# Mixer of the last two blocks: three PSUM pools of two banks merged into one of six used in turn, scores of the differential attention two blocks ahead

## The chip, the cores and the metric

The kernel runs on one core of one Trainium2 chip. The metric is the device time of one execution in microseconds. TensorE multiplies matrices and writes into PSUM (eight banks of 128 x 512 fp32 numbers in this kernel); VectorE, ScalarE and GpSimd read the banks or work on SBUF; SyncE issues most of the DMAs.

## What is computed

Four transformer blocks on 512 tokens of width 1024 in fp32: two of a first kind (window attention with a gated linear attention, then retention) and two of a second kind. The change touches the mixer of the second kind, which runs twice. It has three branches beside each other: a convolution of 31 taps with a norm, a differential attention of six heads, and a gated delta rule of six heads in two directions. Cut to these:

```python
def diff_attention(q, k, v, lam..., subln_w, layer_idx):
    def block(args):                      # 128 queries against 512 keys
        s = jnp.einsum("bqmd,bkmd->bmqk", q_blk, kf)          # 2 x 6 maps, width 32
        p = jax.nn.softmax(s - slopes[:, None, None] * dist, axis=-1)
        p = p.reshape(B, H, 2, Q_BLOCK, S)
        a = p[:, :, 0] - lam * p[:, :, 1]
        return jnp.einsum("bhqk,bkhe->bqhe", a, vf)
    o = rms_norm_2(lax.map(block, ...), subln_w, eps=1e-5) * (1.0 - lambda_init)

def chunk_gated_delta(q, k, v, g, beta):  # chunks of 64 tokens
    A = jnp.where(strict, jnp.einsum("bhncd,bhnsd->bhncs", kb, kc) * decay, 0.0)
    sol = lax.linalg.triangular_solve(A, rhs, left_side=True, lower=True, unit_diagonal=True)
    u, w = sol[..., :Dv], sol[..., Dv:]
    def step(state, inp):
        v_new = u_i - jnp.einsum("bhcd,bhde->bhce", w_i, state)
        o = jnp.einsum("bhcd,bhde->bhce", qg_i, state) + jnp.einsum("bhcs,bhse->bhce", aqk_i, v_new)
        state = state * gl_i[..., None, None] + jnp.einsum("bhcd,bhce->bhde", kdec_i, v_new)
        return state, o

def second_block(x, ...):                 # for l in range(2)
    u = rms_norm_2(x, pre_mix_w[l]) @ w_in[l]                 # then split into the branches
    y = jnp.concatenate([conv_module(...), diff_attention(...), gated_deltanet(...)], axis=-1) @ w_out[l]
    x = x + rms_norm_2(y, post_mix_w[l])
    y = jnp.square(jax.nn.relu(rms_norm_2(x, pre_mlp_w[l]) @ w_ff1[l])) @ w_ff2[l]
    x = x + rms_norm_2(y, post_mlp_w[l])
```

## The kernel before

A product in fp32 is made of three: both operands are split into a high and a low part, and `mm3` issues high x high, high x low and low x high (lines 485 to 487). `wsplit` makes the two parts of a weight (tiles `wh` and `wl`); the split input is `hh` and `hl`. All rows of L485 to L487 are such dense products.

`second(l)` (line 1974) writes the mixer of one layer out as a program, and a tile scheduler makes the five engines' queues from it. The tiles of a pool share its buffers by tag: a tile may be written when an earlier one of its tag has been read for the last time, and tiles of one tag take the buffers in the order of the program. Beyond that an engine's queue can hold a later part of the program ahead of an earlier one. Before, the eight PSUM banks are four pools of two:

- `mm` (`psum`): dense products, the value products of the attention (`L509 mm<-dv,dat`), and the transposes after its norm (L1707).
- `fx` (`psf`): half of the gate projection, the transposes of the short convolution (L1400), and the attention's scores and transposes.
- `ax` (`psx`): everything of the delta rule but its running states, and the transposes of its output (also L1707).
- `sA`: the two running states of a scan.

The program of a mixer, with heads of the delta rule taken in three pairs f = 0, 1, 2:

1. The first projections and `gates`, then for each pair `delta_proj` (its q, k, v), `delta_prep` (products of keys, L1475, with decays, L1446 and L1463; the small triangular systems, `delta_solve`, 15 steps of two VectorE instructions on L1518 and L1520), and its second half, `rest`, on the queries. With them stand the projection and the 31 taps of the convolution (L1743, VectorE).
2. `uw(f)`: the 64 x 64 systems are built from the small ones. For each direction it is a chain TensorE, VectorE, TensorE and so on: L1559 and L1569/L1570 (32 x 32 products), L1571, L1583, an eviction, L1592, L1593, L1583 and L1592 again for the other half, then L1604 (products with values, 64 x 128).
3. `scan(f)`: 7 steps in each direction, a pair of 64 x 64 products into `sA` and a copy (L1650 on VectorE, L1652 on ScalarE) each, then the output's products (all on L509).
4. `out(f)`: a norm over VectorE, ScalarE and GpSimd, four transposes (L1707), an eviction and a DMA.
5. Dense projections of gate and values for tokens (`dense_tok`, 384 columns) and of the attention's q and k (`diff_proj`, 512 columns). The gate projection holds four accumulators at once, `banks = [psum, psum, psf, psf]`, and its weight stays split until the last of the four has used it.
6. `diff`: 24 blocks (six heads by four blocks of 128 queries). `scores(b)` writes two `fx` tiles (L1840), which VectorE takes out with the bias (L1842) and ScalarE exponentiates (L1844). `outputs(b)` combines the two maps (L1854 to L1862; the large step in two blocks of three on VectorE), transposes the result into a third `fx` tile (L1866), copies it out, and multiplies with the values into `mm`. Before, the loop is `scores(b + 1)` then `outputs(b)`. After every second head stand a norm and L1707; after the first of these the convolution's norm.

The order of the program is: proj 0, prep 0, rest 0, proj 1, prep 1, rest 1, projection of the convolution, uw 0, proj 2, taps, prep 2, scan 0, uw 1, gate projection, value projection, q and k projections, out 0, scan 1, rest 2, uw 2, out 1, scan 2, out 2, diff. After it the output projection `w_out` reads all branches.

Of the kernel before, what the change touches and what calls it, by code (L numbers as in the profile page):

```python
# [16 lines left out]
PSUM = bass.MemoryType.PSUM  # L17
# [104 lines left out]
class Rows:  # L122


    def __init__(self, a, b, c0=0, c1=768):
        self.t, self.c0, self.c1 = (a, b), c0, c1
# [32 lines left out]
class Slots:  # L159
# [6 lines left out]
    def tile(self, shape, dt, tag, name, bufs=1):  # L166
        n = int(np.prod(shape[1:]))
        if n < P:
            return self.pool.tile(shape, dt, tag=tag, name=name, bufs=bufs)
        t = self.slots[self.n % len(self.slots)][:, :n]  # L170
        self.n += 1
        names = "abcd"[:len(shape) - 1]
        return t.rearrange(f"p ({' '.join(names)}) -> p {' '.join(names)}", **dict(zip(names, shape[1:])))


class Kern:
# [1618 lines left out]
    def diff(self, l, pool, qk, vd, cat, between):  # L1795
# [31 lines left out]
        def scores(b):  # L1827
            hd, qb = b // 4, b % 4
            if qb == 0:
                head(hd)  # L1830
            s = heads[hd]
            if b % 2 == 0:
                blocks[b // 2] = (self.p_raw.tile([P, 2048], F32, tag="raw", name="dP").rearrange("p (q m c) -> p q m c", q=2, m=2),
                                  self.p_whl.tile([P, 1024], F32R, tag="wl", name="dat").bitcast(F32).rearrange("p (q k c) -> p q k c", q=2, k=4))
            pe = blocks[b // 2][0][:, b % 2]
            o0 = 384 - P * qb
            for m in range(2):
                ps = self.psf()
                t = s["qk"][m]
                nc.tensor.matmul(ps, t[:, qb * P:(qb + 1) * P], t[:, 512:], start=True, stop=True)  # L1840
                mx = s["mx"][:, qb, m:m + 1]
                nc.vector.tensor_tensor_reduce(out=pe[:, m], in0=ps, in1=s["bias"][:, o0:o0 + 512], scale=1.0, scalar=3.0e38,  # L1842
                                               op0=ALU.add, op1=ALU.min, accum_out=mx)
                nc.scalar.activation(pe[:, m], pe[:, m], AF.Exp, bias=mx, scale=-1.0, accum_out=s["sm"][:, qb, m:m + 1])  # L1844
            self.load["dve"] += 1300
            self.load["act"] += 1050
# [33 lines left out]

        nb = 24
        scores(0)
        for b in range(nb):
            if b + 1 < nb:
                scores(b + 1)
            outputs(b)

    def second_consts(self, pool, tmp):
# [85 lines left out]
    def second(self, l):  # L1974
        tc, nc, I = self.tc, self.nc, self.I
# [6 lines left out]
        qk = [pd.tile([2, 4, P, 512], F32, tag=f"qk{l}{f}", name="qk") for f in range(3)]  # L1982
        cat = pd.tile([P, KT, 512], F32, tag=f"cat{l}", name="cat")
        p_ps = ExitStack()
        self.pd, self.pf, self.px, psa = (p_ps.enter_context(tc.tile_pool(name=f"{t}{l}", bufs=2, space=PSUM))
                                          for t in ("mm", "fx", "ax", "sA"))
        p_cv, cv, p_hs = self.p_cv, self.cv, self.p_hs
        nc.sync.dma_start(xs, self.x)
        self.p_x.close()
# [2 lines left out]
        pool = p_dl.enter_context(tc.tile_pool(name=f"dl{l}", bufs=1))  # L1992
# [61 lines left out]
        with ExitStack() as st:  # L2054
# [24 lines left out]
            for k in range(KT):  # L2079
                t = p_f.tile([P, 4, 256], F32, tag="o", name="ct", bufs=2).rearrange("p a b -> p (a b)")[:, :512]  # L2080
# [20 lines left out]
    def mlp(self, l, pool, hs, y, evy, done):  # L2101
# [66 lines left out]
        for p in range(3, 16):  # L2168
            strassen(p)
            if p % 2 == 0 and p < 13:  # L2170
                second([p - 2, p - 1])
# [190 lines left out]
```

## Time and profile before

| what | us |
|---|---|
| median of 3 runs (lowest to highest) | 4025.6 (4014.26 to 4031.81) |
| the profiled execution | 4036.42 |
| its span | 4034.6 |
| first mixer, transpose of the gate rows to first product of the output projection | 420.2 |
| second mixer, the same | 418.3 |

Over the span TensorE is busy 92%, VectorE 60%, GpSimd 41%, ScalarE 39%. The line PEclk of the page cuts the span into 40 slices and shows the clock that TensorE was granted in tenths of its full speed of 2.4 GHz; a stretch with 0.50 is at the lower level of 1.2 GHz all the time, one with 0.75 half of it. In tables of stretches each engine has its busy time in us and, behind x, its instructions; PEld is the loading of weights into TensorE, which runs beside the products. Products are pipelined, so the durations of single ones overlap, and busy time is what counts for many in a row. Where a row names a releaser (`<-PE fx L1840`), it is what ended the idle time of the engine before these instructions.

### The profile page before, as it was taken

The page shows a single profiled execution, that of the slowest core. Times are in us where ns is not written, and L with a number is a line of the kernel's source. Part 1 is how long each engine was busy: PE and PEld are TensorE (multiplying, and loading weights), DVE is VectorE, ACT ScalarE, POOL GpSimd, SP SyncE. Part 2 cuts the span into 40 slices and gives each one's busy share as a digit, 9 for nine tenths or more (in the row PEclk, how much of TensorE's full clock was granted, in tenths as well). Part 3 has the DMA queues.
Part 4 walks back from the last instruction along what each step waited for, and adds up shares of the span by engine and source line. Part 5 has one row for each costly group of instructions (what it writes and reads, how often), then busy time and mean ns, then how long its engine had stood idle before and what let it go on. Part 6 is the DMA issues. An engine that isn't in the chain of part 4 may idle for free. (4 is left out here: it accounts for less than half of the span.)

```text
span 4034.6 us, 67160 instructions
## 1 busy us (share of the span) xinstructions
PE 3704.7 (92%) x27441; PEld 3287.6 (81%) x27441; DVE 2440.8 (60%) x4507; ACT 1571.0 (39%) x2654; POOL 1669.0 (41%) x1168
## 2 busy tenths in 40 slices
PE   8999989989998999997999988878999988878998
PEld 6888767989998788887999876768988776778988
DVE  6454566665666333336776684548767685558665
ACT  4544255323223222223343543444434443344433
POOL 2221225455553223233666454215554363115654
PEclk8999879989999999998999987879999887878999
DMA  6322444112222212121232433132334333132333
GB/s 208 93 77 78 155 130 157 43 53 65 72 73 77 66 58 71 60 84 51 84 115 88 118 99 119 52 113 94 105 105 122 92 101 104 55 123 92 105 97 112
DMA packets 420364, 379.79 MB, mean 94 GB/s; under 512 B 64586, under 2 KB 366169, under 8 KB 419161
## 3 DMA queue, kind: packets, MB, share of 16 engines
q1 hardware_dynamic: 414490, 367.01, 29.4%
q10 hardware_dynamic: 5567, 8.49, 0.6%
q8 instruction: 216, 3.54, 0.4%
q14 instruction: 91, 0.75, 0.1%
HBM read 332.21 MB, written 43.25 MB: 93 GB/s over the span
## 5 line engine op out<-in xcount | busy, mean ns | idle before, releaser
L206 ACT CAST wh<-raw 128x1024 fp32r<-128x1024 f32 (+2 forms) x441 | 444.6, 1014 | 630.9 <-PE mm L486 277.6
L233 POOL TENSOR_TENSOR wl<-raw,wh 128x1024 fp32r<-128x1024 f32 (+2 forms) x196 | 468.1, 2397 | 530.7 <-ACT wh L206 476.5
L233 DVE TENSOR_TENSOR wl<-raw,wh 128x1024 fp32r<-128x1024 f32 (+1 forms) x268 | 378.1, 1415 | 189.1 <-ACT wh L206 176.4
L485 PE MATMUL mm<-Hh,wh 128*128 128x512 f32 (+1 forms) x1256 | 417.5, 335 | 15.3 <-DVE x L1033 12.9
L487 PE MATMUL mm<-Hh,wl 128*128 128x512 f32 (+1 forms) x1256 | 417.0, 333 | 0.5 <-DVE wl L233 0.5
L486 PE MATMUL mm<-Hl,wh 128*128 128x512 f32 (+1 forms) x1256 | 416.3, 332 | 0.0
L485 PEld LDWEIGHTS mm<-Hh,wh 128*128 128x128 f32 x1256 | 238.7, 190 | 42.9 <-DVE x L1033 14.3
L487 PEld LDWEIGHTS mm<-Hh,wl 128*128 128x128 f32 x1256 | 238.8, 190 | 26.1 <-DVE wl L233 0.7
L486 PEld LDWEIGHTS mm<-Hl,wh 128*128 128x128 f32 x1256 | 239.0, 190 | 24.3
L485 PE MATMUL mm<-hh,wh 128*128 128x512 f32 (+1 forms) x640 | 231.9, 366 | 16.4 <-DVE hh L208 6.9
L509 PE MATMUL mm<-hl,wh 128*128 128x256 f32 (+1 forms) x808 | 231.5, 290 | 6.4 <-DVE hl L1960 6.3
L509 PE MATMUL mm<-hh,wl 128*128 128x256 f32 (+1 forms) x808 | 231.6, 290 | 5.5 <-DVE wl L233 4.1
L487 PE MATMUL mm<-hh,wl 128*128 128x512 f32 (+1 forms) x640 | 227.2, 357 | 2.8 <-POOL wl L233 2.8
L486 PE MATMUL mm<-hl,wh 128*128 128x512 f32 (+1 forms) x640 | 229.0, 359 | 0.6 <-DVE hl L698 0.6
L509 PE MATMUL mm<-hh,wh 128*128 128x256 f32 (+1 forms) x808 | 218.4, 288 | 6.5 <-ACT hh L1968 3.2
L206 ACT CAST wh<-s 128x1024 fp32r<-128x1024 f32 (+1 forms) x128 | 106.9, 835 | 267.4 <-PE mm L486 137.6
L509 PE MATMUL mm<-th,wh 128*128 128x256 f32 (+1 forms) x644 | 195.3, 305 | 8.1 <-ACT wh L206 5.5
L509 PE MATMUL mm<-th,wl 128*128 128x256 f32 (+1 forms) x644 | 197.3, 307 | 3.1 <-DVE wl L233 3.1
L1033 DVE SCALAR_TENSOR_TENSOR x<-mm,mod,x 128x512 f32<-128x512 f32 (+1 forms) x224 | 138.2, 630 | 99.9 <-PE mm L487 99.4
L509 PE MATMUL mm<-tl,wh 128*128 128x256 f32 (+1 forms) x644 | 195.3, 303 | 0.6 <-DVE tl L233 0.6
L233 POOL TENSOR_TENSOR Hl<-o,Hh 128x1024 fp32r<-128x1024 f32 (+3 forms) x76 | 140.9, 1856 | 92.6 <-ACT Hh L206 91.1
L509 PEld LDWEIGHTS mm<-hl,wh 128*128 128x128 f32 (+1 forms) x808 | 155.8, 193 | 9.7 <-DVE hl L1960 7.7
(737 smaller groups left out, 10886.8 us busy)
## 6 DMA issues: line engine op xcount, KB each, us to landing
raw<-in_w_ff_dram SPq DMA_DIRECT2D x68, 1024.0 KB
raw<-in_ffn_w_in_dram SPq DMA_DIRECT2D x88, 512.0 KB
raw<-in_mod_w_dram SPq DMA_DIRECT2D x40, 1024.0 KB
raw<-in_odd_w_in_dram SPq DMA_DIRECT2D x24, 1024.0 KB
raw<-in_ffn_w_out_dram SPq DMA_DIRECT2D x19, 1024.0 KB
raw<-in_w_in_dram SPq DMA_DIRECT2D x38, 512.0 KB
dqk<-qk SPq DMA_DIRECT2D x48, 256.0 KB
raw<-in_w_out_dram SPq DMA_DIRECT2D x12, 768.0 KB
```

Of the source, the lines that this page charges most:

```text
L206: nc.scalar.copy(hi, src)
L233: i = (nc.vector if e == "dve" else nc.gpsimd).tensor_tensor(out=out, in0=a, in1=b, op=op)
L485: mm(ps, ah, bh, start=first, stop=False)
L486: mm(ps, ah, bl, start=False, stop=False)
L487: mm(ps, al, bh, start=False, stop=last)
L509: i = self.nc.tensor.matmul(out, lhsT, rhs, start=start, stop=stop, skip_group_check=True)
L1033: self.nc.vector.scalar_tensor_tensor(out=x[:, ct, :n], in0=ps, scalar=gate[:, ct:ct + 1], in1=x[:, ct, :n], op0=ALU.mult, op1=ALU.add)
```

## The change

In `second(l)` the pools `fx`, `ax` and `sA` are gone. One pool `any` of six banks takes their place, and the class `OneTag` gives all tiles from `psf`, `psx` and the scan's `sA` the same tag, so that the six banks are used in turn by all of them. `mm` keeps its two. In `diff` the scores are issued two blocks ahead of the outputs. No instruction is added or taken away but seven of ScalarE's table loads.

```diff
+class OneTag:
+    def __init__(self, pool):
+        self.pool = pool
+
+    def tile(self, shape, dt, tag, name):
+        return self.pool.tile(shape, dt, tag="any", name=name)
...
         nb = 24
         scores(0)
+        scores(1)
         for b in range(nb):
-            if b + 1 < nb:
-                scores(b + 1)
+            if b + 2 < nb:
+                scores(b + 2)
             outputs(b)
...
-        self.pd, self.pf, self.px, psa = (p_ps.enter_context(tc.tile_pool(name=f"{t}{l}", bufs=2, space=PSUM))
-                                          for t in ("mm", "fx", "ax", "sA"))
+        self.pd, ps = (p_ps.enter_context(tc.tile_pool(name=f"{t}{l}", bufs=n, space=PSUM)) for t, n in (("mm", 2), ("any", 6)))
+        self.pf = self.px = psa = OneTag(ps)
```

The new class lies ahead of all else, so a line of before has a number that is 10 higher after the change (11 higher behind line 1890). The names of tiles (`fx`, `ax`, `sA`) stay what they were. An `x8` behind an instruction of an order means eight of that kind in a row.

**First place: the gate projection on TensorE.** Before, its two `fx` accumulators begin among the key products of pair 1 (L1475) and the short convolution's transposes (L1400):

```order
L1475 MATMUL ax<-kT 64x64 x8
L1400 MATMUL fx<-ident,pc 128x128 x4
L487 MATMUL mm<-wh,hl 128x384
L1475 MATMUL ax<-kT 64x64 x8
L485 MATMUL fx<-wh,hh 128x384
L486 MATMUL fx<-wl,hh 128x384
L487 MATMUL fx<-wh,hl 128x384
```

After, the `fx` accumulators begin behind the last steps of uw 1:

```order
L1593 MATMUL ax<-TZ,KK 32x32 x8
L1602 MATMUL ax<-Z,Q 32x32 x8
L1593 MATMUL ax<-TZ,KK 32x32 x8
L1602 MATMUL ax<-Z,Q 32x32 x8
L1614 MATMUL ax<-VB,Z 64x128 x2
L495 MATMUL fx<-wh,hh 128x384
L496 MATMUL fx<-wl,hh 128x384
L497 MATMUL fx<-wh,hl 128x384
```

The `fx` half moved behind the chain of uw 1, and with it 144 products of 384 columns and 144 of 512 that come after it in the queue.

**Second place: the chain of a uw step on TensorE.** Before, in uw 2 of the first mixer, scores (L1840), transposes (L1866) and value products (`mm<-dv,dat`) of the attention stand between its products:

```order
L1583 MATMUL ax<-TZ,KK 32x32 x8
L509 MATMUL mm<-dv,dat 128x64 x4
L1840 MATMUL fx<-dqk 128x512
L1866 MATMUL fx<-ident,dP 128x128 x4
L1592 MATMUL ax<-Z,Q 32x32 x8
L1583 MATMUL ax<-TZ,KK 32x32 x8
L1840 MATMUL fx<-dqk 128x512
L509 MATMUL mm<-dv,dat 128x64 x4
L1840 MATMUL fx<-dqk 128x512
L1592 MATMUL ax<-Z,Q 32x32 x8
L1604 MATMUL ax<-VB,Z 64x128
```

After, a uw step's products follow each other:

```order
L1593 MATMUL ax<-TZ,KK 32x32 x8
L1602 MATMUL ax<-Z,Q 32x32 x8
L1593 MATMUL ax<-TZ,KK 32x32 x8
L1602 MATMUL ax<-Z,Q 32x32 x8
L1614 MATMUL ax<-VB,Z 64x128 x2
L1569 MATMUL ax<-TZ,A_22859 32x32 x13
L1614 MATMUL ax<-VB,Z 64x128 x14
```

The attention's rows are gone from between the steps; only the next direction's first products (L1569, L1559 of before) still stand among the last ones.

**Third place: where the attention begins on TensorE.** Before, the first scores stand between the last dense products of q and k and the last step of uw 0, ahead of the preparation of pair 2 and the first scan:

```order
L485 MATMUL mm<-hh,wh 128x512
L486 MATMUL mm<-hl,wh 128x512
L487 MATMUL mm<-hh,wl 128x512
L1840 MATMUL fx<-dqk 128x512 x2
L1592 MATMUL ax<-Z,Q 32x32 x8
L1604 MATMUL ax<-VB,Z 64x128 x16
L1431 MATMUL ax<-ident,tokk 128x128 x4
L1446 MATMUL ax<-gd,dm 128x512
L509 MATMUL sA<-U,kd 64x64 x14
L1840 MATMUL fx<-dqk 128x512 x2
```

After, they stand behind the third scan's last products and the transposes of its output:

```order
L519 MATMUL ax<-U,Aq 64x64 x15
L519 MATMUL ax<-kd,qg 64x64 x28
L1717 MATMUL ax<-ident,OI 128x128 x4
L1850 MATMUL fx<-dqk 128x512 x6
L1876 MATMUL fx<-ident,dP 128x128 x4
L1850 MATMUL fx<-dqk 128x512 x2
L1876 MATMUL fx<-ident,dP 128x128 x4
L1850 MATMUL fx<-dqk 128x512 x2
L519 MATMUL mm<-dv,dat 128x64 x4
```

All 48 scores of a mixer moved behind the delta rule, and from then on the scores of one block stand behind each block's transposes. At the end, the value products of the last eight blocks stand behind the convolution's norm.

## Rows read from the trace of the kernel before

**Rows 1.** Page, 40 slices of the span: TensorE's granted clock, in tenths.
```profile
PEclk8999879989999999998999987879999887878999
```

**Rows 2.** Stretches of the first mixer: us, engines' busy time, granted clock, DMA.
```profile
2267.30:2389.20 121.90, 105.76 (x579) 87.00 (x579) 104.31 (x195) 69.64 (x102) 64.40 (x42) 0.90 0.38 98
2389.20:2455.10 65.90, 61.42 (x768) 51.12 (x768) 33.34 (x62) 23.10 (x37) 38.60 (x27) 0.95 0.45 140
2455.10:2479.40 24.30, 17.53 (x136) 11.12 (x136) 15.49 (x31) 11.04 (x23) 9.32 (x8) 0.72 0.59 184
2479.40:2503.00 23.60, 19.12 (x378) 18.19 (x374) 11.38 (x45) 4.36 (x13) 2.54 (x2) 0.63 0.21 41
2503.00:2549.60 46.60, 36.59 (x687) 30.34 (x684) 26.32 (x70) 16.45 (x38) 15.28 (x13) 0.73 0.18 52
2549.60:2570.00 20.40, 17.53 (x407) 16.09 (x406) 12.28 (x37) 7.70 (x21) 4.63 (x4) 0.79 0.15 43
2570.00:2613.30 43.30, 39.57 (x765) 32.71 (x762) 29.39 (x86) 21.92 (x53) 9.55 (x8) 0.88 0.16 55
2613.30:2629.00 15.70, 14.04 (x390) 13.70 (x390) 6.83 (x27) 4.73 (x14) 2.31 (x2) 0.89 0.13 44
2629.00:2687.50 58.50, 36.99 (x164) 30.63 (x164) 33.40 (x107) 25.33 (x48) 5.42 (x6) 0.57 0.37 126
sum 420.20, PE 348.54 PEld 290.89 DVE 272.73 ACT 184.27 POOL 152.06; mean PE 38.73 PEld 32.32 DVE 30.30 ACT 20.47 POOL 16.90
```

**Rows 3.** Stretches of the second mixer: first scan, third scan, the sum.
```profile
3376.80:3401.20 24.40, 16.83 (x372) 15.93 (x366) 11.36 (x45) 4.04 (x11) 2.54 (x2) 0.71 0.21 40
...
3510.60:3524.60 14.00, 12.51 (x389) 12.19 (x388) 6.75 (x27) 4.76 (x14) 2.32 (x2) 1.00 0.14 49
...
sum 418.30, PE 345.12 PEld 287.34 DVE 271.11 ACT 184.18 POOL 151.97; mean PE 38.35 PEld 31.93 DVE 30.12 ACT 20.46 POOL 16.89
```

**Rows 4.** Stretches within the first mixer: dense 512, dense 384, VectorE full, its end.
```profile
2327.10:2337.80 10.70, 10.52 (x46) 8.20 (x45) 10.14 (x25) 6.37 (x9) 4.71 (x4) 1.00 0.41 124
2389.80:2395.60 5.80, 5.80 (x46) 5.51 (x34) 5.76 (x9) 2.29 (x4) 4.76 (x3) 1.00 0.47 127
2334.00:2389.20 55.20, 42.49 (x243) 37.38 (x242) 54.74 (x82) 29.84 (x44) 34.52 (x24) 0.81 0.28 65
2671.80:2687.50 15.70, 2.19 (x10) 1.61 (x9) 5.88 (x20) 2.67 (x4) 2.30 (x2) 0.50 0.50 165
```

**Rows 5.** One line: taps of the convolution, minimum, median and maximum in ns.
```profile
L1743 DVE SCALAR_TENSOR_TENSOR cacc<-hp,dw,cacc x30: 735/752/2862, 2331.5 to 2395.9; 128x512 f32<-128x512 f32 x30
```

**Rows 6.** VectorE's groups, 2455.1 to 2687.5: busy us, mean ns, idle before.
```profile
L1842 DVE CUSTOM_DVE_ANT_0 dP<-fx,abias 128x512 f32<-128x512 f32 x48 | 32.5, 686 | 11.2 <-PE fx L1840 10.1 <-POOL abias L1809 0.6
L1862 DVE SCALAR_TENSOR_TENSOR dP<-dP,drs 128x512 f32<-128x512 f32 x16 | 14.2, 885 | 0.4
...
L1593 DVE TENSOR_SCALAR Z<-ax 32x256 f32<-32x256 f32 x9 | 3.8, 421 | 3.7 <-PE ax L1592 3.6
...
L1518 DVE TENSOR_TENSOR chT<-chG,chX 128x15 f32<-128x15 f32 (+7 forms) x15 | 3.1, 205 | 2.5 <-DMA chG<-gdd 2.0
```

**Rows 7.** TensorE's groups, 2570.0 to 2613.3, eight blocks of attention within.
```profile
L509 PE MATMUL mm<-dv,dat 128*128 128x64 f32 x64 | 9.8, 298 | 0.0
L1840 PE MATMUL fx<-dqk 128*128 128x512 f32 x16 | 8.2, 530 | 0.0
...
L1866 PE MATMUL fx<-ident,dP 128*128 128x128 f32 x32 | 5.5, 299 | 1.4 <-DVE dmx L1842 1.2 <-DVE dP L1862 0.2
```

**Rows 8.** TensorE's timeline at the first mixer's end: start, us, instruction.
```profile
2664.52 0.77 PE L1840 MATMUL fx<-dqk 128*128 128x512 f32 x1
...
2669.17 1.06 PE L1866 MATMUL fx<-ident,dP 128*128 128x128 f32 x4
2670.91 1.97 PE L509 MATMUL mm<-dv,dat 128*128 128x64 f32 x8 [0.68 <-ACT dat L243]
2682.95 1.12 PE L1707 MATMUL mm<-ident,do 128*128 128x128 f32 x4 [10.07 <-POOL do L233]
```

## The prediction

> **What bounds the kernel now.** I read the page's slices first: the clock that TensorE is granted sinks in slices 24 to 27 and 32 to 37, which hold the attention halves of the two mixers and what follows them [rows 1]. Then I cut the first mixer into nine stretches, from the transpose of the gate rows (2267.3 us) to the first product of the output projection (2687.5): 420.2 us, in which TensorE is busy 348.5 and idle about 70. The second mixer takes 418.3 us [rows 2, 3]. The change writes nothing outside the mixers, so its effect lies in these 838 us.
>
> Two regimes are to be seen. Up to 2455 us the dense projections cover the delta rule's chains: TensorE has 0.90 to 0.95 of its clock, and its idle time falls where VectorE is full (54.7 of 55.2 us) [rows 2, 4]. From 2455 on there are no dense products; the 24 blocks of the differential attention and the delta chains (two pairs of uw steps and three scans) share the queues, at 0.57 to 0.89 of the clock [rows 2]. What covers a chain's waits there is the attention. The last stretch is attention nearly alone: 58.5 us for its last six blocks and the closing norm [rows 2].
>
> **What the change does to the order.** Before, scores and transposes of the attention (fx) had two banks of their own, so they could be taken ahead of delta tiles (ax, sA) that the program writes earlier. With one pool of six used in turn, a tile waits for the turn of those written before it. The order shows three consequences, in each mixer:
> 1. No score stands among the delta rows any more. All 48 come behind the last scan and its output transpose (third place shown in the change).
> 2. Of the gate projection's four accumulators two are of mm and two of fx. The fx half now stands behind the second uw pair, and until it is done the split weights stay held, so 144 products of 384 columns and 144 of 512 that stood inside the chains before now stand in one run behind it (first place).
> 3. The uw pairs and scans stand with next to nothing between their steps (second place).
>
> **The sum, stretch by stretch, for the first mixer.**
>
> Start to the first uw row, 121.9 us before. 150 products leave it, 126 of 384 columns at 5.8 us for 32 (14 short products of a chain among them) and 24 of 512 at 10.7 us for 44 (and two short ones) [rows 4]: 28.7 us of TensorE, so 93 us are left if every stall stays. VectorE's rows ahead of the same point fall by 27 us (20 convolution taps of 0.75 us [rows 5], four weight splits and others) from 101 to 74, which is the floor. Between 74 and 93 I take 84, because VectorE was the full engine.
>
> First uw pair and preparation of the third head pair, 90.2 us before (stretches two and three). 210 dense products stood there, 66 of 384 columns and 144 of 512 (47 us); now 72 (14.5 us). That leaves 57.7 us. About 5 us of attention leave as well, and VectorE's rows between the two landmarks come to 48 us, 23 taps among them, as floor; single taps took up to 2.86 us before [rows 5]. Ends 48 and 62; I take 56.
>
> First scan, 23.6 us before, 24.4 in the second mixer; the third scan took 15.7 and, in the second mixer, 14.0 [rows 2, 3]. The solve's 30 small VectorE steps still stand between its copies, and their first still waits for a DMA [rows 6]. Ends 14 and 24; I take 21, near its own rows.
>
> A uw pair alone: stretch six, 43.3 us, holds a pair, the query products and eight blocks of attention, which cost TensorE 9.8 + 8.2 + 5.5 = 23.5 us [rows 7]. Without them 19.8 us are left if no wait is uncovered. Each of the two directions has five evictions in series (0.42 us in the row of L1593 [rows 6], and the way to and back); at 0.85 us uncovered, ten add 8.5. I take 28 us for this stretch and 23.5 for the other pair (46.6 before), which has no query products. Ends for a pair: 18, and 33 if hardly anything of the attention's share comes back.
>
> Dense run, new in its place: 144 x 0.181 + 144 x 0.243 = 61 us, 64 with a start. These products were counted out above.
>
> Output of head pair 0: its tiles need the space of the dense source, so it starts when the run ends, and the second scan's bank comes after it in turn. Nothing covers it. The nearest row is the same norm at the mixer's end, which leaves TensorE idle 10.1 us [rows 8]. I take 9, ends 7 and 12; for pair 2, ahead of the first score, 9.5.
>
> Second and third scan, 20.4 and 15.7 us before: 15.5 and 15.
>
> Attention alone, in place of the 58.5 us. Three blocks of scores stand ahead at the start, and one follows each transpose. VectorE needs per block 2 x 0.69 + two thirds of 0.89 = 2.0 us in its large rows [rows 6]; TensorE 2.9 at 0.88 clock [rows 7] and 2 x 0.77 + 1.06 + 1.97 = 4.6 at half clock [rows 8]. With one block ahead and two banks the last six blocks took about 43 us, 7 each. Now no bank is short; I take 3.3 us, with 2.6 and 4.4 as ends. That is 79 us, and 2 to start. Then what follows: eight blocks of value products stand behind the convolution's norm, at 1.2 to 1.97 us each [rows 7, 8], 12.5 in all; 3 for the rest of that norm; and from the last value product to the output projection 15.7 us [rows 4]. Together 112.
>
> Sum: 84 + 56 + 21 + 23.5 + 64 + 9 + 15.5 + 28 + 15 + 9.5 + 112 = 437.5 us against 420.2: +17.3, and +19 in the second mixer (418.3). Seven table loads of ScalarE leave the program, off the path. The profiled execution's 4036.4 becomes 4072.7; the median of the runs is 10.8 us below that execution, so **4062 us**.
>
> A rule of the Trainium skill speaks against the change: Perfetto Trace Analysis, section Optimization Strategy, says that a kernel with several regimes may gain from interleaving them. Here it agrees: a uw pair and eight blocks stand together in 43.3 us, of which 23.5 are the blocks' [rows 2, 7].
>
> **Rivals.**
> *The faster attention just pays for the lost cover* (no change, 4026 us): 17 us a mixer are less than the terms' uncertainty; at 2.6 us a block instead of 3.3 they are gone. For it: VectorE's 2.0 us. Against it: TensorE's 2.9 to 4.6.
> *VectorE bound both regimes* (faster, 3982 us): without the attention's share of its queue, the first two terms run at their floors (74 and 48 us, 18 less), the attention at 2.6 us a block (17 less) and the pairs 2 us shorter each: 39 us below my sum, 22 a mixer below before. It decides if a block takes under 2.7 us. Against it: from 2455 us on VectorE is busy 58% and TensorE 78% [rows 2]. The Trainium skill's page Perfetto Trace Analysis, section Matmuls, wants independent groups to rotate through different PSUM banks; that rule is on this rival's side, and the 7 us a block with two banks agree with it.
> *The bare chains run at the lower clock* (slower, 4124 us): scans at 0.63 and 0.71 clock took 23.6 and 24.4 us, at 0.89 and 1.00 15.7 and 14.0 [rows 2, 3], and in the stretch with the idle time at the end the clock was 0.50 [rows 4]. If all that is bare runs there, two scans cost 8 us more each, the pairs and the norms' transposes 8 together, the attention 3.6 instead of 3.3: 31 us a mixer more.
> *The tiles don't take turns*, and the order stays: excluded, since the order shows the scores behind the scans.
>
> **How the numbers follow.** Forecast (4040 to 4090 by its own terms) 0.44; no change 0.21; lower clock 0.19; VectorE's relief 0.16. About 20 us (0.5%) is what a measurement of this kernel can tell. The forecast's lower edge touches that band, so a little of its share counts as no change: faster 0.15, same 0.25, slower 0.60. With all ends taken low a mixer would lose 40 us, with all high it would grow by 100; that all go one way is unlikely. The range of 3990 to 4135 leaves out about a tenth on each side.
>
> **What would show it.** Right: no score ahead of the third scan; dense products in one run of 60 to 66 us near full clock; TensorE idle 8 to 10 us ahead of two output transposes; uw pairs of 20 to 28 us; attention from first score to output projection 105 to 120 us; mixers of 428 to 450 us. Wrong: blocks at 2.7 us or less, or mixers below 415 us (the cover was worth less than the rows say), or scans of 20 us and more at half clock (the price is the clock, not the waits).

## The result and the profile after

The changed kernel takes 4182.4 us in the median (4179.1 to 4188.9 in four runs), the kernel before 4025.3: a ratio of 1.0395 with a 95% interval of 1.0369 to 1.0422. It is slower by 157 us. The direction was forecast; the forecast was +36 us, and the time lies above the range of 3990 to 4135. The nearest rival, the lower clock, had forecast 4124.

The page's first part, before and then after; each engine has its busy time, its share of the span and its instructions:

```profile
PE 3704.7 (92%) x27441; PEld 3287.6 (81%) x27441; DVE 2440.8 (60%) x4507; ACT 1571.0 (39%) x2654; POOL 1669.0 (41%) x1168
```

```profile
PE 3707.4 (89%) x27441; PEld 3306.9 (79%) x27441; DVE 2436.3 (58%) x4507; ACT 1560.2 (37%) x2647; POOL 1665.2 (40%) x1168
```

The span of the two profiled executions grew from 4034.6 to 4177.3 us, by 142.7, and TensorE's busy time by 2.7. (That is less than 157 us because the profiled execution before lies 11 us above its median and the one after 3 us below.) So nearly all of the loss is time in which TensorE is idle; its products as a whole did not get slower, which already speaks against the rival of the lower clock. The two mixers, cut at the same landmarks as before, took 493.4 and 483.6 us instead of 420.2 and 418.3 [rows 2, 3]: 138 us of the 143.

The first mixer after, in stretches (us, then busy time of TensorE, weight loads, VectorE, ScalarE and GpSimd, granted clock, DMA share, GB/s). They begin with the transpose of the gate rows, the first uw row, the first scan, uw 1, the dense run without delta products between, its end, the transposes of out 0, the start of rest 2, the transposes of out 1, the end of scan 2, and the first score:

```profile
2269.70:2355.30 85.60, 71.59 (x419) 54.84 (x421) 66.42 (x141) 41.68 (x63) 39.38 (x29) 0.94 0.39 97
2355.30:2432.90 77.60, 45.82 (x699) 38.02 (x702) 67.30 (x113) 30.41 (x51) 46.17 (x34) 0.71 0.18 43
2432.90:2463.90 31.00, 20.75 (x436) 19.46 (x433) 15.96 (x48) 8.90 (x19) 13.25 (x11) 0.67 0.17 32
2463.90:2495.90 32.00, 25.64 (x594) 22.99 (x594) 11.09 (x18) 3.37 (x8) 8.11 (x7) 0.63 0.09 11
2495.90:2551.90 56.00, 55.94 (x272) 48.85 (x271) 8.97 (x10) 16.11 (x23) 10.62 (x5) 1.00 0.53 173
2551.90:2569.60 17.70, 0.03 (x1) 0.03 (x1) 4.71 (x17) 1.11 (x2) 4.19 (x4) 0.58 0.71 239
2569.60:2585.40 15.80, 15.80 (x421) 15.29 (x422) 4.61 (x11) 3.58 (x10) 0.00 (x0) 0.82 0.12 41
2585.40:2614.20 28.80, 19.78 (x585) 17.37 (x585) 12.30 (x33) 2.98 (x7) 4.39 (x4) 0.68 0.04 12
2614.20:2631.60 17.40, 17.38 (x449) 16.81 (x448) 3.32 (x9) 4.87 (x14) 0.00 (x0) 0.85 0.05 18
2631.60:2639.10 7.50, 0.77 (x5) 0.80 (x5) 4.80 (x17) 1.22 (x2) 0.00 (x0) 0.83 0.00 1
2639.10:2763.10 124.00, 80.74 (x399) 72.46 (x397) 77.15 (x245) 63.95 (x144) 21.96 (x20) 0.64 0.28 98
sum 493.40, PE 354.24 PEld 306.93 DVE 276.61 ACT 178.19 POOL 148.06; mean PE 32.20 PEld 27.90 DVE 25.15 ACT 16.20 POOL 13.46
```

TensorE is busy 354.2 us where it was 348.5 [rows 2]; it is idle 139 us where it was 72. The dense run is the one stretch without a gap (55.9 of 56.0 us, at the full clock), and right behind it stands the one with nothing at all (0.03 of 17.7). The first 18 dense products already stand among the last ones of uw 1 (from 2488.8 us on), so uw 1 alone takes about 25 us and the dense run 63; the table has the two together. Set against the prediction's sum, with the second mixer beside it:

| stretch | before | forecast | after | second mixer after |
|---|---|---|---|---|
| to the first uw row | 121.9 | 84 | 85.6 | 85.1 |
| uw 0, preparation of pair 2 | 90.2 | 56 | **77.6** | 80.6 |
| scan 0 | 23.6 | 21 | **31.0** | 26.6 |
| uw 1 and the dense run | 46.6 | 87.5 | 88.0 | 87.5 |
| out 0 and scan 1 | 20.4 | 24.5 | **33.5** | 33.8 |
| rest 2 and uw 2 | 43.3 | 28 | 28.8 | 28.8 |
| out 1 and scan 2 | 15.7 | 15 | 17.4 | 17.2 |
| out 2 | none | 9.5 | 7.5 | 7.5 |
| attention alone, closing norms | 58.5 | 112 | **124.0** | 116.5 |
| sum | 420.2 | 437.5 | 493.4 | 483.6 |

Four terms carry 53 of the 56 us by which the first mixer exceeds its forecast. What each waits for is read with the experiments.

### The profile page after: what moved, and what is told of

Its sections match the earlier page's. It is cut to its first block, busy times and chain, and to the rows that moved or that the text cites. A ratio compares the mean times of both kernels' runs of the same rounds, so it can differ in the third digit from the quotient of the medians.

```text
span 4177.3 us, 67214 instructions
## 1 busy us (share of the span) xinstructions
PE 3707.4 (89%) x27441; PEld 3306.9 (79%) x27441; DVE 2436.3 (58%) x4507; ACT 1560.2 (37%) x2647; POOL 1665.2 (40%) x1168
## 5 line engine op out<-in xcount | busy, mean ns | idle before, releaser
L495 PEld LDWEIGHTS mm<-Hh,wh 128*128 128x128 f32 x1256 | 238.7, 190 | 41.9 <-DVE x L1043 13.1
L495 PEld LDWEIGHTS mm<-hh,wh 128*128 128x128 f32 x640 | 123.6, 194 | 53.4 <-DVE pc L1404 8.4
```

What stands on the lines that cost most here:

```text
L495: mm(ps, ah, bh, start=first, stop=False)
```

## Experiments: which sharing costs

Theory A is the prediction's: the tiles of fx wait their turn behind delta tiles, so the attention and the dense products no longer cover the delta chains. Theory B: the two states of a scan hold two of the six banks and stop the turn for everything. Theory C: scores two blocks ahead crowd the shared banks. "In one line" means that tiles take the banks of one pool in turn. All ratios below are to the kernel before on the same chip.

**Scores one block ahead, with the pool of six** (e1_merge_only)

```diff
         scores(0)
-        scores(1)
         for b in range(nb):
-            if b + 2 < nb:
-                scores(b + 2)
+            if b + 1 < nb:
+                scores(b + 1)
             outputs(b)
```

> The pool of six as in the changed kernel, scores one block ahead as before. Theory A (lost cover: attention and half the gate projection wait their turn behind the delta chains): the time stays at that of the changed kernel, 4182 us, within 20 us. Theory B (the two running states of a scan, held long, block the turn) says the same of this run. Theory C (two blocks ahead is what costs, by crowding the shared banks): most of the 157 us come back, 4030 to 4080 us.

Measured: 4190.7 us, ratio 1.0391 (1.0365 to 1.0417), the same as the whole change. Theory C falls.

**Scores two blocks ahead, with the four pools of before** (e2_two_ahead_only; the edit is the loop alone)

> The four pools of two banks as before, scores two blocks ahead. Theories A and B: two banks of fx hold one block of scores, so the order hardly changes: 4026 us within 20. Theory C: 4080 us or more.

Measured: 4019.8 us, ratio 0.9974 (0.9960 to 0.9989): if anything a quarter of a per cent faster than before. Nothing of the loss comes from this part of the change.

**Only ax and sA in turn; fx keeps its two banks** (e3_fx_apart, one block ahead)

```diff
-        self.pd, ps = (... for t, n in (("mm", 2), ("any", 6)))
-        self.pf = self.px = psa = OneTag(ps)
+        self.pd, self.pf, ps = (... for t, n in (("mm", 2), ("fx", 2), ("any", 4)))
+        self.px = psa = OneTag(ps)
```

> Only ax and sA merged (four banks in turn); fx keeps its two, scores one block ahead. Theory A: the attention and the gate projection stand among the delta rows again, so the time is back at 4026 us within 40, and may fall below by the second pair of banks that a uw chain gains (down to 3990). Theory B (held states block the turn of the delta chains' own tiles): 4100 us or more.

Measured: 4043.5 us, ratio 1.0033 (1.0018 to 1.0047). Almost all is back. The hope of a gain from the second pair of banks for the delta chains did not come true.

**Only fx and ax in turn; the states keep their two banks** (e4_sA_apart, one block ahead)

```diff
-        self.pd, ps = (... for t, n in (("mm", 2), ("any", 6)))
-        self.pf = self.px = psa = OneTag(ps)
+        self.pd, psa, ps = (... for t, n in (("mm", 2), ("sA", 2), ("any", 4)))
+        self.pf = self.px = OneTag(ps)
```

> Only fx and ax merged (four banks in turn); the scan's states keep their two, scores one block ahead. Theory A: all scores still stand behind the last scan and half the gate projection behind the second pair of uw steps: 4140 to 4200 us. Theory B: back at 4026 us within 40.

Measured: 4178.5 us, ratio 1.0362 (1.0334 to 1.0390). Theory B falls, and the number of banks in turn does not make the loss: with six or with four it is alike. What costs is that fx stands in one line with ax.

**The gate projection out of the line, the attention in it** (e5_gate_apart)

```diff
-        self.pd, ps = (... for t, n in (("mm", 2), ("any", 6)))
+        self.pd, pz, ps = (... for t, n in (("mm", 2), ("gz", 2), ("any", 4)))
         self.pf = self.px = psa = OneTag(ps)
...
-        banks = [self.psum, self.psum, self.psf, self.psf]
+        psz = lambda: pz.tile([P, 512], F32, tag="gz", name="gz")
+        banks = [self.psum, self.psum, psz, psz]
```

> As the changed kernel, but the gate projection's second two accumulators have two banks of their own (the shared pool has four); the attention stays behind the last scan. If the dense run behind the second uw pair is a cost because its products no longer fill the idle time of TensorE in the chains before (32 us in the stretch of the first uw pair, 16 in the first scan and second pair, per mixer), some 25 to 45 us a mixer come back: 4090 to 4130 us. If VectorE alone sets the length there, the dense run does not shrink either and it stays at 4160 to 4185.

Measured: 4125.8 us, ratio 1.0255 (1.0235 to 1.0275), 57 us back. Its first mixer takes 457.3 us. The stretch of the first uw pair, and the one from uw 1 to the transposes of out 0, same columns as above:

```profile
2369.80:2447.40 77.60, 62.15 (x809) 55.90 (x810) 65.08 (x106) 33.41 (x55) 51.17 (x35) 0.82 0.25 60
...
2476.60:2533.50 56.90, 46.42 (x705) 37.68 (x704) 22.09 (x40) 9.18 (x18) 16.40 (x13) 0.95 0.51 167
```

The uw stretch is exactly as long as in the changed kernel, 77.6 us, but TensorE does 62.2 us of work in it instead of 45.8, and behind it 56.9 us do what took 32.0 + 56.0 + 17.7 = 105.7. So the dense products there fill idle time at no cost in that stretch, though the stretch ahead of it is 11 us longer (97.0 against 85.6). VectorE is the fullest engine in both kernels (65.1 and 67.3 of 77.6 us); whether it sets the length is tested below.

**The attention out of the line, the gate projection in it** (e6_attention_apart)

```diff
-        self.pd, ps = (... for t, n in (("mm", 2), ("any", 6)))
+        self.pd, pf, ps = (... for t, n in (("mm", 2), ("fx", 2), ("any", 4)))
         self.pf = self.px = psa = OneTag(ps)
...
+        self.pf = pf
         self.diff(l, rb, qk, vd, cat, ...)
```

> The complement: scores and transposes of the attention have two banks of their own, the gate projection's second half and the delta rule share four. If the cost is the attention that stands alone (124 and 117 us a mixer behind the third scan against 58 and 61 before), most of it comes back although the dense run stays: 4060 to 4110 us. If the held gate projection is the larger part: 4120 to 4170. Together with the run before, the two gains should add to the 139 us between the changed kernel and the one with fx wholly apart, if they are independent.

Measured: 4141.3 us, ratio 1.0287 (1.0253 to 1.0321), 41 us back: the second case, the held gate projection is the larger part. With the 57 of the run before it is 98 us, not 139.

**Both out of the line, two blocks ahead** (e13_fx_apart_two_ahead; e3's pools with the changed loop)

> fx wholly apart with its two banks, ax and sA in turn on four, scores two blocks ahead: the sum of the two kernels that took out only the gate projection (4126 us) and only the attention (4141 us), with everything else as in them. If the two costs are independent, this is 4182 - 57 - 41 = 4085 us. If each hole was partly covered by what the other edit brought back, and only both together restore the cover, it stands where its twin with one block ahead stood (4043), less the 5 to 10 us that two ahead gave elsewhere: 4030 to 4045.

Measured: 4026.6 us, ratio 0.9996 (0.9979 to 1.0013). Everything is back, 156 us, some 58 more than the two runs before give together. A part of the reason shows in one line of four traces, the loads of a mixer's 48 scores (minimum, median and maximum in ns, then the first and last start in us). Before:

```profile
L1840 PEld LDWEIGHTS fx<-dqk x48: 186/192/338, 2454.9 to 2664.5; 128*128 128x128 f32 x48
```

The changed kernel:

```profile
L1850 PEld LDWEIGHTS fx<-dqk x48: 186/330/338, 2639.0 to 2718.9; 128*128 128x128 f32 x48
```

Only the attention out of the line:

```profile
L1850 PEld LDWEIGHTS fx<-dqk x48: 186/287/338, 2537.4 to 2697.7; 128*128 128x128 f32 x48
```

Both out:

```profile
L1850 PEld LDWEIGHTS fx<-dqk x48: 185/193/338, 2487.2 to 2647.5; 128*128 128x128 f32 x48
```

Counted from each mixer's start the first score comes 188, 369, 276 and 221 us in. The attention reads the projections of q and k, which the program has behind the gate projection; while that one is held, banks of its own help the attention only from 276 us on, when uw 0, scan 0 and uw 1 are over. So the two costs hang together: the gate projection holds the dense work, and the dense work holds the attention.

That all of the 58 us come from this is not shown, since this run takes out a third thing as well. The transposes of the short convolution are fx tiles too, and in the two runs before they stay in the line. The last of a mixer's 36 starts here 9 us after the first uw row (26 us ahead of it in the kernel before), but 60 us after it in the changed kernel, and 59 and 53 us in the two runs before; the preparation of pair 2 needs them. First the changed kernel, then this run:

```profile
L1410 PE MATMUL fx<-ident,pc x36: 272/417/473, 2291.5 to 2415.4; 128*128 128x128 f32 x36
L1410 PE MATMUL fx<-ident,pc x36: 270/273/475, 2276.0 to 2370.1; 128*128 128x128 f32 x36
```

No run takes these transposes out alone.

**Three banks for fx, three for ax and sA** (e11_fx3_any3, two ahead)

```diff
-        self.pd, ps = (... for t, n in (("mm", 2), ("any", 6)))
-        self.pf = self.px = psa = OneTag(ps)
+        self.pd, self.pf, ps = (... for t, n in (("mm", 2), ("fx", 3), ("any", 3)))
+        self.px = psa = OneTag(ps)
```

> Three banks for fx, three in turn for ax and sA, two for mm, scores two blocks ahead. By the lost-cover theory the attention stands among the delta rows and has a third bank; with two of the three shared banks held by a scan's states, a delta chain has one left while a scan runs. Gain of the third fx bank against loss in scans: 4000 to 4050 us. If a scan's held states cost the chains more: 4060 to 4120.

Measured: 4049.2 us, ratio 1.0053 (1.0039 to 1.0068), the upper end of the first case. Against two banks for fx and four in turn (0.9996) a third bank for the attention does not pay for the one that the delta rule loses.

## Experiments: the terms that were too small

**The taps.** The convolution has two halves of 30 taps each behind the first. VectorE does the taps of one half (L1743, L1753 after the change); of the other, ScalarE scales each tap (L1756) and GpSimd adds it (L1757). In the uw stretch the chain of the second direction waits at one place 9.5 us. VectorE's timeline there, rows left out (start, us, instruction, idle time ahead of it):

```profile
2394.79 0.42 DVE L1575 COPY AT<-ax 128x256 f32<-128x256 f32 x1 [0.45 <-PE ax L1569]
2395.13 0.56 DVE L1528 TENSOR_TENSOR chT<-chG,chX 128x64 f32<-128x64 f32 x1
2395.61 1.55 DVE L1753 SCALAR_TENSOR_TENSOR cacc<-hp,dw,cacc 128x512 f32<-128x512 f32 x1
2397.08 1.06 DVE L1530 TENSOR_TENSOR chX<-chX,chT 128x64 f32<-128x64 f32 x1
...
2404.30 1.26 DVE L1528 TENSOR_TENSOR chT<-chG,chX 128x55 f32<-128x55 f32 x1
2405.49 0.68 DVE L1581 TENSOR_TENSOR TZ<-TZ,ax 128x512 f32<-128x512 f32 x1
```

and TensorE's row that follows:

```profile
2406.21 1.06 PE L1593 MATMUL ax<-TZ,KK 32*32 32x32 f32 x16 [9.49 <-DVE TZ L1581]
```

Between two evictions of the chain (L1575 and L1581) VectorE's queue holds taps of the convolution (L1753) and steps of the triangular solve of pair 1 (L1528, L1530), the second of the mixer's three. The products that L1581 takes out were done 1.5 us after L1575; the queue came to L1581 only at 2405.49. So taps were left out, first VectorE's half (e7_after_no_taps), then both (e9_after_no_conv), and both in the kernel before as well (e14_before_no_conv):

```diff
-            for t in range(1, 31):
+            for t in range(1, 31 if z else 2):     # e7; range(1, 2) in e9 and e14
```

> The changed kernel with VectorE's 30 taps of the convolution's first half left out (ScalarE's and GpSimd's half is kept). The stretch from the first uw row to the first scan took 77.6 us where 56 were forecast, and VectorE is busy 67.3 of it, 27.3 with taps. If VectorE's queue sets its length, it falls to 50 to 58 us and the kernel to 4130 to 4150. If the bare chain sets it (matrix steps and evictions in series at a low clock), the stretch stays over 68 us and the kernel over 4160.

> The changed kernel with 30 of 31 taps of the convolution left out in both halves (VectorE's, and those that ScalarE scales and GpSimd adds). Without VectorE's half the stretch from the first uw row to the first scan was 67 and 65 us (78 and 81 with it; 56 forecast), and its longest wait, 10.1 us, was for a norm whose square stood in ScalarE's queue behind taps that wait for GpSimd. If the taps in the in-order queues are what lengthens the chain, the stretch falls to 48 to 58 us and the kernel to 4100 to 4130. If the bare chain is that long by itself, the stretch stays over 62 and the kernel over 4135.

> The kernel before with 30 of 31 taps of the convolution left out in both halves, to be set beside the changed kernel with the same left out (4128 us; 54 us less than with them). If the taps in the queues are a cost of the bare chain alone, the kernel before loses little without them, 4005 to 4025 us, and the change costs 105 to 120 us instead of 157. If they cost the same under cover (VectorE was full in the first stretch, 54.7 of 55.2 us), 3970 to 3995 and the change costs 135 to 157 with or without them.

Measured: 4146.8 us without VectorE's half (ratio 1.0314, 1.0289 to 1.0339) and 4128.2 without both (1.0246, 1.0227 to 1.0265). The uw stretch of the first mixer in these two, same columns as above:

```profile
2355.20:2422.30 67.10, 46.88 (x694) 37.46 (x696) 41.02 (x88) 30.49 (x50) 43.74 (x35) 0.72 0.20 46
```

```profile
2355.70:2410.50 54.80, 43.20 (x697) 34.49 (x699) 34.22 (x88) 15.85 (x29) 14.02 (x12) 0.76 0.25 57
```

77.6, 67.1 and 54.8 us: VectorE's half is worth 10 us of the stretch, which ends between the two cases of the first expectation (the kernel's time lies in the first), and the other half 12, the first case of the second. In the first of the two kernels the next wait is on ScalarE's queue, by the waits of that stretch (who waits for whom: us in total, times, longest):

```profile
ACT cm L1756 <- POOL cacc L1757: 23.1, 16, 4.0
...
PE ax L1441 <- DVE tokk L243: 10.1, 1, 10.1
DVE dss L1428 <- ACT dsq L1427: 9.2, 2, 8.9
```

ScalarE scales a tap into the one buffer `cm` and must wait until GpSimd has added the one before; the square of a norm (L1427) stands in ScalarE's queue behind that, VectorE waits for the square and TensorE for VectorE. Without any taps the stretch takes 54.8 and, in the second mixer, 57.2 us: the forecast's 56. How much of the other half's 12 us is this queue, and how much the steps of the solve, which also became shorter (last section), is not separated.

Before loses less by the taps: 3994.8 us without them (ratio 0.9925, 0.9896 to 0.9955), 34 us less than with them where the changed kernel saves 54. That is the second case, at its edge: the change still costs 133 us without taps. Most of the taps' cost lay on the path before too, and some 20 to 30 of the 157 us are what they cost more in the changed kernel.

**The stores behind the dense run.** The 17.7 us ahead of out 0's transposes, VectorE, GpSimd and TensorE:

```profile
2562.55 0.69 DVE L1796 SCALAR_TENSOR_TENSOR dlo<-mm,dhi 128x512 fp32r<-128x512 f32 x1 [9.31 <-DMA qk<-dhi]
2563.16 0.67 DVE L1705 TENSOR_REDUCE hss<-hsq 128x8 f32<-128x512 f32 x1
...
2566.41 1.04 POOL L243 TENSOR_TENSOR OI<-OI,hy 128x512 f32<-128x512 f32 x1 [4.14 <-DVE hy L655]
...
2569.57 1.12 PE L1717 MATMUL ax<-ident,OI 128*128 128x128 f32 x4 [17.73 <-POOL OI L243]
```

The norm's first step on VectorE (L1705) stands behind the last eviction of the q and k projections (L1796), and that waits 9.3 us for a buffer, which a store must free. Five buffers instead of three:

```diff
-                    hi = pool.tile([P, 512], F32, tag="pc", name="dhi", bufs=3)
+                    hi = pool.tile([P, 512], F32, tag="pc", name="dhi", bufs=5)     # and the other four tiles of the tag
```

> The changed kernel with five buffers instead of three for what the projections put into SBUF on its way out (tag pc). Behind the dense run TensorE is idle 17.7 us where 9 were forecast: VectorE's last eviction there waits 9.3 us for a store, and the norm of out 0 stands behind it. If that store is the cause, the gap falls to about 9 us in each mixer and the kernel to 4160 to 4172; if the norm itself takes that long, nothing changes (4175 to 4190).

Measured: 4192.8 us, ratio 1.0418 (1.0399 to 1.0437): no gain, so the store is not the one cause. The gap is 16.4 us. VectorE's wait for the store is shorter (5.2 us), and GpSimd now waits for two loads of the same time:

```profile
2557.57 0.69 DVE L1796 SCALAR_TENSOR_TENSOR dlo<-mm,dhi 128x512 fp32r<-128x512 f32 x1 [5.16 <-DMA qk<-dhi]
```

```profile
2565.52 1.95 POOL L1819 TENSOR_SCALAR abias<-dist 128x896 f32<-128x896 f32 x2 [33.53 <-DMA dist<-in_k_dist_dram]
2567.55 1.04 POOL L243 TENSOR_TENSOR OI<-OI,hy 128x512 f32<-128x512 f32 x1
2571.76 1.26 POOL L243 TENSOR_TENSOR OI<-OI,zt 128x512 f32<-128x512 f32 x1 [3.16 <-DMA zt<-zd]
```

The norm's step on GpSimd now stands behind the attention's bias, whose table is still being loaded, and then waits for its own gate rows. In this gap of the changed kernel the DMA engines move 239 GB/s at a share of 0.71, more than in any other stretch of the mixer: before, shares of 0.45 and 0.59 lay over 90 us that other work filled [rows 2]; now the projections' transfers land where the dense products end and nothing else is left to do. That these transfers together make the gap as long as it is, is read from the trace; no run without them tests it.

**The convolution's norm.** In the changed kernel 80.4 us pass from the first to the last score, 32.0 from there to the last value product, 11.6 to the output projection. In both kernels the convolution's norm is written behind the norm of the second head pair (`f == 1`). Here it was written behind the first one's:

```diff
-        self.diff(..., lambda f: self.conv_norm(l, rb, acc, cat) if f == 1 else None)
+        self.diff(..., lambda f: self.conv_norm(l, rb, acc, cat) if f == 0 else None)
```

> The changed kernel with the convolution's norm written behind the first norm of the attention instead of the second, so that its two tiles take the mm banks earlier. In the changed kernel 32 us pass from the last score to the last value product, half of them the norm's steps with 64 value products queued behind. If the held value products are a cost of their own, the stretch behind the third scan falls from 124 and 117 to 105 to 112 us and the kernel to 4150 to 4170. If they only wait instead of something else, it stays at 4175 to 4190.

Measured: 4189.0 us, ratio 1.0395 (1.0375 to 1.0415): nothing gained. The first two of these pieces in its first mixer:

```profile
2638.60:2733.90 95.30, 66.99 (x314) 58.49 (x312) 62.09 (x209) 56.94 (x129) 15.78 (x15) 0.64 0.25 86
2733.90:2749.10 15.20, 11.14 (x81) 10.56 (x80) 10.53 (x18) 7.11 (x14) 3.94 (x3) 0.74 0.41 138
```

The 32 us behind the last score became 15, and the 80 ahead of it 95. So the norm costs some 16 us at both places in an attention that nothing covers.

**The gain that was left.** Two blocks ahead in the pools of before, with the norm early (e12_two_ahead_norm_early):

> The four pools of before, scores two blocks ahead, and the convolution's norm behind the first norm of the attention. Two ahead alone gave 0.9974 of before. If the norm's mm tiles delay value products at the end there too (58 us for the last six blocks and the norm), another 5 to 10 us a mixer: 4000 to 4012 us. If the norm then stands among the delta chains and lengthens those, 4020 to 4040.

Measured: 4029.4 us in 12 runs, ratio 1.0004 (0.9992 to 1.0017), the second case by its time. The best version of this study stays the loop alone, 0.9974.

## Why the prediction was wrong

**Right: the mechanism, the direction and the order.** No score stood ahead of the third scan, the dense products ran at the full clock in one piece, and the three runs e3, e4 and e13 show that fx and ax in one line, and not the number of banks, make the loss. These terms came out: the start (85.6 against 84), uw 1 with the dense run (88.0 against 87.5), the third uw pair (28.8 against 28, worked out from the seventh row of [rows 2], there called stretch six), the second scan itself (15.8 against 15.5), out 2 (7.5 against 9.5), the third scan (17.4 against 15), and the attention's blocks, 80.4 / 24 = 3.35 us against 3.3. The start came out near its term without the reason given for it: VectorE was busy 66.4 us there, below the 74 that were called its floor. Of the signs named, the order, the dense run and the blocks held; the mixers (493 and 484 us against 428 to 450) and the idle time ahead of out 0 (17.7 against 8 to 10) did not.

**Wrong: the step of the first uw pair and the preparation, "Ends 48 and 62; I take 56"** (+21.6 us, and +24.6 in the second mixer; above its own high end). The floor of 48 us was VectorE's rows there, and VectorE was busy 67.3. Its 26 taps took 1.05 us each, and the solve's 30 steps 13.7 us. Both prices were to be had before: the median of the taps was 0.75 us, but their mean 1.09, and a solve's steps took 6.2 us only where GpSimd adds no taps [rows 6]; in the mixer's first part two solves took 25.9 us. VectorE's rows there (2267.3 to 2480 us, busy us, mean ns, idle before):

```profile
L1743 DVE SCALAR_TENSOR_TENSOR cacc<-hp,dw,cacc 128x512 f32<-128x512 f32 x30 | 32.8, 1094 | 0.7 <-ACT cacc L1739 0.6
...
L1518 DVE TENSOR_TENSOR chT<-chG,chX 128x15 f32<-128x15 f32 (+7 forms) x30 | 13.5, 449 | 1.6 <-DMA chG<-gdd 1.3
L1520 DVE TENSOR_TENSOR chX<-chX,chT 128x15 f32<-128x15 f32 (+7 forms) x30 | 12.4, 414 | 0.3
```

So these instructions did not get slower by the change; the prediction named the taps' maximum of 2.86 us [rows 5] and priced a tap at 0.75. The other part of the error goes with the other half's taps: a queue that I did not look at (ScalarE's taps, each waiting for GpSimd, ahead of a norm's square) and the solve's longer steps. Without the taps of both halves the stretch took the 56 us of the forecast (54.8 and 57.2).

**Wrong: scan 0, 21 forecast** (+10.0 and +5.6, above its high end of 24). I took the row of before, which had a wait of 2.0 us for the solve's DMA in VectorE's queue [rows 6]. VectorE's rows after:

```profile
2440.55 0.27 DVE L1660 COPY kd<-sA 64x128 f32<-64x128 f32 x1
...
2446.18 0.87 DVE L1528 TENSOR_TENSOR chT<-chG,chX 128x15 f32<-128x15 f32 x1 [5.35 <-DMA chG<-gdd]
...
2449.20 0.29 DVE L1660 COPY kd<-sA 64x128 f32<-64x128 f32 x1
```

The scan follows the key products at once, so the solve's first step waits 5.4 us for its input and the scan's next copy stands behind it: 8.7 us between two copies, where the same two were 2.3 us apart before (2487.99 and 2490.29 us). That is 6.4 of the 7.4 us by which this scan is longer than before. Even without taps it took 27 us, and TensorE waited 6.0 us in it for a step of the solve. No run tests it by itself, so why the input comes later is open.

**Wrong: out 0, "I take 9, ends 7 and 12"** (+8.7). The nearest row was a norm whose step on VectorE stood behind a wait of 1.6 us for a load, beside a DMA share of 0.50 [rows 4, 8]; here it stood behind 9.3 us for a store, beside 0.71. The prediction had moved 61 us of dense products in front of out 0 and not their stores, although it had counted the products out one by one. The trace shows the wait for a store; with more buffers the gap stayed, with loads in its place. Which transfers would have to go to have 9 us is open.

**Wrong: "3 for the rest of that norm"** (+12 in that stretch). The closing norm of the convolution costs 16 us there, by the run with the norm early. In the 58.5 us of before I had counted it as part of "7 us a block", and so gave it to the two banks.

**The range** was worked out as if the terms erred independently ("that all go one way is unlikely"), but these four were all too low together. In uw 0, scan 0 and out 0 the price counted too little of what stands ahead of the chain's steps in an engine's queue; the norm's price counted 3 of its 16 us. The terms' own high ends made +100 us a mixer; the truth was +73 and +65. That this sum covers the truth is luck, since the first three lie above their own high ends.

**The rivals.** That the faster attention pays for the lost cover fell: 3.35 us a block left nothing over. That VectorE was the bound and would be relieved is right in its first half in one stretch only, with the opposite sign: in that of uw 0 VectorE was fuller than before (67.3 of 77.6 us), and leaving out its taps gave 10 us back. The lower clock fell as a net cost: TensorE's busy time rose by 5.7 us in the first mixer and fell by 1.2 in the second, where before it was 345.12 [rows 3] and after 343.90. The bare second and third scans ran at 0.82 and 0.85 in 15.8 and 17.4 us, not at the lower level. On the Trainium skill's two rules (Perfetto Trace Analysis): that of the section Optimization Strategy, that interleaving regimes may improve performance, is what this case bears out, with 139 idle us in a mixer without it and 72 with it. That of the section Matmuls, that independent groups should rotate through different banks, is not against it: in one line the turn itself made the groups dependent (1.0362 to 1.0395 against 0.9996 apart).

## What to carry to other kernels

A pool that is used in turn is a queue: a tile waits for the turn of those written before it, so two streams of work that should fill each other's gaps need pools of their own, even if each then has fewer banks (here two and four instead of six). When a change takes cover away, price each bare chain by the in-order queues of all the engines it passes (what else stands in them, and for what that waits), not by its own steps at median durations from a quieter place, and let the errors of such terms add up in the range. And count the stores and loads that move with a block of products: here the busiest stretch of the DMA engines came right behind it.

## What the runs showed of the hardware

VectorE's small steps stretched to the end of an addition on GpSimd. A solve step of 0.2 us (L1528) took 1.28, 1.27 and 1.27 us at 2382.41, 2385.06 and 2402.20 us in the changed kernel; an addition of GpSimd was running at each, and the step ended within 0.1 us of it. In the uw stretch the step's mean is 646 ns, and with its partner L1530 the 30 steps of a solve take 13.7 us:

```profile
L1528 DVE TENSOR_TENSOR chT<-chG,chX 128x15 f32<-128x15 f32 (+7 forms) x15 | 9.7, 646 | 0.1
```

Without VectorE's taps, but with GpSimd's, the 30 steps still take 13.1 us (5.9 here and 7.2 in L1530):

```profile
L1528 DVE TENSOR_TENSOR chT<-chG,chX 128x15 f32<-128x15 f32 (+7 forms) x15 | 5.9, 395 | 2.1 <-DMA chG<-gdd 1.7
```

Without the taps of both halves they take 7.1 us (4.0 and 3.1), so it is the half of ScalarE and GpSimd that stretches them:

```profile
L1528 DVE TENSOR_TENSOR chT<-chG,chX 128x15 f32<-128x15 f32 (+7 forms) x15 | 4.0, 264 | 3.2 <-DMA chG<-gdd 2.7
```

The Trainium skill's page SBUF — State Buffer, section SBUF: two separate sides, describes a port pair of these two engines as a lock that one of them holds for a whole instruction while the other waits; these rows agree with it. It is a second reason why a median from a quiet stretch is too low for a busy one.
